# One inference step of a two-layer hybrid decoder: the dt projection made from raw rows, among the first tiles' products

## The chip, the cores and the metric

The kernel runs on one core of a Trainium2 chip. Its time is the device time of one execution in microseconds (us); the time shown is the median of three runs, 936.38 us, with a lowest of 936.22 and a highest of 937.31.

The engines are named as in the profile: PE is the matrix engine and PEld its weight loads, DVE the vector engine, ACT the scalar (activation) engine, POOL the third elementwise engine, SP the queue that issues most transfers. Each engine works through its own instructions in the order in which they stand in its queue, and waits there for semaphores of the others.

## The reference, cut to what matters

The model has one state-space layer (Mamba-2 SSD, mixer A) and one dilated-attention layer (mixer B). 512 prompt rows and 8 x 4 sample rows, 544 in all, of width 1024 go through both. The change lies at the start of mixer A:

```python
u = rmsnorm(h, g_norm) @ w_in
z      = u[..., :SSM_INNER]                        # 2048 columns
xbc    = u[..., SSM_INNER:SSM_INNER + CONV_DIM]    # 3072 columns: x, B, C
dt_raw = u[..., SSM_INNER + CONV_DIM:]             # 32 columns, one per head
...                                                # causal conv over xbc, silu
dt = softplus(dt_raw + dt_bias)
a  = -exp(a_log)
y, s_final = ssd_scan(xs * dt[..., None], dt * a, bm, cm, ssm_init)
```

`rmsnorm(x, g)` is `x * rsqrt(mean(x*x) + eps) * g`. Its first factor is one number per row, so a product with a weight may be made from `x * g` (raw rows) and multiplied by that number afterwards. The scan needs `dt` of all heads before its first chunk of 128 rows: every decay in it comes from sums of `dt * a`.

## The kernel before, in words

Activations lie transposed: 128 of the 1024 features on the partitions, eight such pieces (k = 0 to 7), and the 544 rows along the free axis. The rows are handled in two halves, columns 0 to 255 and 256 to 543 (256 prompt rows and the 32 sample rows). A weight tile is 1024 x 128. Each product is made in three passes of a rounded format to keep the precision of full floats: the weight is split into `whi` (ACT, L205 or L440) and `wlo` = raw - `whi` (DVE, L206 or L444), the rows into a high and a low part, and PE sums `whi` x high, `whi` x low and `wlo` x high. One tile is so 24 products for each half.

**The first five tiles** (16, 20 and 0 of the x|B|C columns, then z 0 and z 1) are made from raw rows, since the norm isn't known yet: `raw(i, ks)` splits `x * g` into `xh` and `xl` (ACT L389, DVE L393), `passes` makes the products, and `scaled_in`, `scaled_in2` and `z_raw` multiply the results by the norm `rs_x`. Squares for the norm are made on ACT (`x_square`), added on DVE (`x_add`), summed over partitions on PE (`x_sums`, the tile `ms`), and the root is spread over the partitions by one more product (`rp`), copied to `rs_x` by ACT. Meanwhile DVE and ACT make the normed rows: `norm(i, ks)` is for each k an `x_mul` (DVE L385, in place: `x` is overwritten by the normed row), an `x_high` (ACT L398, `nh`) and an `x_low` (DVE L402, `nl`). **All later tiles** are made from `nh` and `nl`. Order is fixed by hand in this stretch: PE's products are pinned, and instructions under `hold` keep their places; the rest is placed by a scheduler with priorities (weight splits have high priority).

**The dt projection** (`dt_proj`, L558 to L566) comes after the fifth tile: for each k, four products of the 1024 x 32 weight `wd` with 128 prompt rows each, and four with 8 sample rows each, in full float format. Group j of rows (j = 0 to 3) goes to partitions 32j to 32j+31 of one PSUM tile `dp`, that is to its own quarter of PE's columns. It reads the normed rows `x` in place, so it needs `x_mul` of both halves. `dt_chain` (L568 to L602) then makes softplus, decays and their exponentials out of `dp` in some 20 small steps of 136 columns on DVE and ACT, writes them to memory (`aed`) and prepares `dgs`, from which PE spreads decays (`spread_decays`, `dx`) and transposes (`tp`, `tq`) inside the stream of tiles.

After that a loop runs over the units of the scan (`ssm_chunk`, `ssm_quad`) while a generator, `filler_a`, feeds the remaining tiles to PE between them: tiles 6, 7 and 8 (x 1, x 2, x 3), then `tok_transposes`, tile 9, and after the first six products of half 0 of tile 10 the first chunk, whose transposes `xp` read the convolved and activated x tiles 0 to 3 (`xs`, DVE L644 and L645 behind ACT's tanh L643). Below, "tile 6" is the first tile from normed rows. PSUM has two rotating pools: `pj` (three banks, for the tiles' sums) and `pss` (five banks, for all else). Weight splits have two buffers each, so `whi` of a tile can be made when PE is through with the tile two before it.

Of the kernel before, what the change touches and what calls it, by code (L numbers as in the profile page):

```python
# [12 lines left out]
F32 = mybir.dt.float32  # L13
F32R = mybir.dt.float32r
AF = mybir.ActivationFunctionType
ALU = mybir.AluOpType
# [3 lines left out]
SEQ = 512  # L20
# [6 lines left out]
KD = D // 128  # L27
# [100 lines left out]
def tile_yoco_step(  # L128
# [6 lines left out]
    nc = tc.nc  # L135
    dma = nc.sync.dma_start
# [6 lines left out]
    hold = tc.keep_in_program_order  # L143

    def mm(*a, **k):
        pin(nc.tensor.matmul(*a, **k))  # L146
# [13 lines left out]
    def pj(name, cols=512):  # L160
        return psum.tile([128, cols], F32, name=name, tag="pj", bufs=3)

    def pss(name, shape=(128, 512)):
        return psum.tile(list(shape), F32, name=name, tag="ss", bufs=5)
# [29 lines left out]
    def fetch_w(src):  # L194
        raw = wpool.tile([128, 8, 128], F32, name="wraw", bufs=3)
        dma(raw, src)
        return raw
# [108 lines left out]
    w_raw = [fetch_w(w_in[0])]  # L306
    load_x(1, 0, HA)
    w_raw.append(fetch_w(w_in[1]))
    for i in range(2):
        load_x(i, HA, T)  # L310
    w_raw.append(fetch_w(w_in[2]))

    x_h = [half("xh0", F32R), half("xh1", F32R)]
    x_l = [half("xl0", F32R), half("xl1", F32R)]
    wd = wk.tile([128, 8, 32], F32, name="wd", bufs=1)
    dma(wd, w_dt)
    dcs = ac.tile([128, 2], F32, name="dcs")
    dma(dcs, dconst)
    tm = half("tm").rearrange("p a b -> p (a b)")
# [38 lines left out]
    xdg = tm[:, 1600:1600 + T]  # L358
    halves = ((0, HA), (HA, T))

    def x_square(i):
        c0, c1 = halves[i]
        for h_ in range(2):
            hold(nc.scalar.activation(sqx[h_][:, :, c0:c1], x_t[h_][:, :, c0:c1], AF.Square))

    def x_add(i):
        s0_, s1_ = (sqx[j][:, :, halves[i][0]:halves[i][1]] for j in range(2))
        hold(nc.vector.tensor_tensor(s0_, s0_, s1_, op=ALU.add))
        hold(nc.vector.tensor_tensor(s0_[:, 0:2], s0_[:, 0:2], s0_[:, 2:4], op=ALU.add))
# [12 lines left out]
    def x_mul(k, i):  # L382
        c0, c1 = halves[i]
        xk = part(x_t, k, c0, c1)
        hold(nc.vector.scalar_tensor_tensor(xk, xk, g_a[:, k:k + 1], rs_x[:, c0:c1], op0=ALU.mult, op1=ALU.mult))  # L385
# [10 lines left out]
    def x_high(k, i):  # L396
        c0, c1 = halves[i]
        hold(nc.scalar.activation(part(n_h, k, c0, c1), part(x_t, k, c0, c1), AF.Copy))  # L398

    def x_low(k, i):  # L400
        c0, c1 = halves[i]
        hold(nc.vector.tensor_tensor(part(n_l, k, c0, c1), part(x_t, k, c0, c1), f32(part(n_h, k, c0, c1)), op=ALU.subtract))  # L402

    def passes(p, w, i, high=True, low=True, between=None):
        c0, c1 = halves[i]
        hi, lo = w
        o = p[:, 0:c1 - c0]
        for k in range(KD if high else 0):
            mm(o, hi[:, k, :], part(x_h, k, c0, c1), start=k == 0, stop=False)
            mm(o, hi[:, k, :], part(x_l, k, c0, c1), start=False, stop=False)  # L410
            if between:
                between(k)
        for k in range(KD if low else 0):
            mm(o, lo[:, k, :], part(x_h, k, c0, c1), start=False, stop=k == KD - 1)
# [21 lines left out]
    def w_high(i):  # L436
        hi = wpool.tile([128, 8, 128], F32R, name="whi", bufs=2)
        lo = wpool.tile([128, 8, 128], F32R, name="wlo", bufs=2)
        w_first[i] = hi, lo
        hold(nc.scalar.activation(hi, w_raw[i], AF.Copy))  # L440

    def w_low(i):
        hi, lo = w_first[i]
        hold(nc.vector.tensor_tensor(lo, w_raw[i], f32(hi), op=ALU.subtract))  # L444

    def raw(i, ks):
        for k in ks:
            x_raw_h(k, i)
            x_raw_l(k, i)

    def norm(i, ks):
        for k in ks:
            x_mul(k, i)
            x_high(k, i)
            if k:
                x_low(k - 1, i)

    def next_raw(i):
        w_raw.append(fetch_w(w_in[i]))
        w_high(i)  # L460

    raw(0, range(4))
    w_high(0)
    raw(0, range(4, KD))
    w_high(1)
    w_low(0)
    w_low(1)
    x_square(0)
    pa, pb = [pj("pa"), pj("pb")], [pj("pa")]
    passes(pa[0], w_first[0], 0, low=False)  # L470
    passes(pa[1], w_first[1], 0, low=False)
    passes(pa[0], w_first[0], 0, high=False)
    passes(pa[1], w_first[1], 0, high=False)
    x_add(0)
# [5 lines left out]
    def spread_a(k):  # L480
        if k == 4:
            hold(nc.scalar.copy(rs_x[:, 0:HA], spread()[:, 0:HA]))

    passes(pb[0], w_first[0], 1, between=spread_a)
    x_square(1)
    cbs = [scaled_in(first[0], pa[0]), scaled_in(first[1], pa[1])]
    x_add(1)
    n_h = [half("nh0", F32R), half("nh1", F32R)]
    n_l = [half("nl0", F32R), half("nl1", F32R)]
    pb.append(pj("pb"))  # L490
    w_high(2)
    norm(0, range(2))
    passes(pb[1], w_first[1], 1)
    sums = x_sums(1)
    spread = rstd_fin(*sums, later=True, keep=hold)
# [50 lines left out]
                x_low(KD - 1, 1)  # L546
    x_h, x_l = n_h, n_l


    t0, t1, t2, t3, t4 = (tm[:, 136 * i:136 * i + 136] for i in range(1, 6))  # L550
    pads = tm[:, 816:1200].rearrange("p (a b) -> p a b", b=128)
    dgs = tm[:, 1200:1584].rearrange("p (a b) -> p a b", b=128)
    tok = ac.tile([128, 6, 3, NH], F32, name="tok")
    dec = ac.tile([128, 12, NH], F32, name="dec")
    nega = ac.tile([128, 1], F32, name="nega")
    dp = [None]

    def dt_proj():  # L558
        dp[0] = pss("dp")
        for k in range(KD):  # L560
            for j in range(4):
                xk = x_t[k // 4][:, k % 4, :]
                o = dp[0][32 * j:32 * j + 32]
                mm(o[:, 0:128], wd[:, k, :], xk[:, 128 * j:128 * j + 128], start=k == 0, stop=False, skip_group_check=True)
                mm(o[:, 128:136], wd[:, k, :], xk[:, SEQ + 8 * j:SEQ + 8 * j + 8], start=False, stop=k == KD - 1,
                   skip_group_check=True)  # L566

    def dt_chain():  # L568
        nc.vector.tensor_scalar(t0, dp[0][:, 0:136], dcs[:, 0:1], None, op0=ALU.add)
        nc.vector.scalar_tensor_tensor(t1, t0, -1.0, t0, op0=ALU.mult, op1=ALU.min)  # L570
        nc.scalar.activation(t2, t1, AF.Exp)
        tc.keep_in_program_order(nc.scalar.activation(nega, dcs[:, 1:2], AF.Exp))
        nc.vector.tensor_scalar(t3, t2, 1.0, None, op0=ALU.add)
        nc.scalar.activation(t1, t3, AF.Ln)
        nc.vector.tensor_scalar(t3, t3, -1.0, 1e-30, op0=ALU.add, op1=ALU.max)
        nc.vector.reciprocal(t3, t3)
        nc.vector.tensor_tensor(t1, t1, t2, op=ALU.mult)
        nc.vector.tensor_tensor(t1, t1, t3, op=ALU.mult)
# [12 lines left out]
        nc.vector.tensor_tensor(t4, t4, t0, op=ALU.mult)  # L591
        t23 = tm[:, 136 * 3:136 * 5].rearrange("p (i c) -> p i c", i=2)
        dma(aed[:].rearrange("i r c -> r i c"), t23[:, :, 0:128])
        dma(sed0[:], t23[:, :, 128:136])
        for i in range(2):
            dma(dap(sed, i * NH * 32, [[32, NH], [8, 4], [1, 8]]), dap(sed0, 8 * i, [[16, NH], [16 * NH, 4], [1, 8]]))
        for i, c in enumerate((127, 131, 135)):
            nc.vector.tensor_scalar(dgs[:, i, :], ident, t3[:, c:c + 1], None, op0=ALU.mult)
        nc.gpsimd.memset(pads, 0.0)
        for i, s in enumerate((t2, t0, t4)):  # L600
            for r in range(2):
                thrice(pads[:, i, 64 * r:64 * r + 64].rearrange("p (b c) -> p b c", c=32), s[:, 128:136])  # L602
# [63 lines left out]
        return xs_t[ti // 4][:, ti % 4, :]  # L666

    def conv_tile(ti, w):
        pa, pb = pj("pa"), pj("pb")
        yield from proj_steps(pa, [w], x_h, x_l, 0, HA)  # L670
        yield from proj_steps(pb, [w], x_h, x_l, HA, T)
        conv(ti, pa[:, 0:HA], pb[:, 0:HB], conv_dst(ti))
# [226 lines left out]
    units = [(f, (g, i)) for g in range(4) for f, i in  # L899
             ((ssm_chunk, 0), (ssm_chunk, 1), (ssm_quad, 0), (ssm_chunk, 2), (ssm_chunk, 3), (ssm_quad, 1))]  # L900
    conv_out(first[0], cbs[0], conv_dst(first[0]))
    dt_proj()
    dt_chain()
    conv_out(first[1], cbs[1], conv_dst(first[1]))
    conv_out(first[2], cbs[2], conv_dst(first[2]))
# [737 lines left out]
    for u in range(len(units) + LA + 2):  # L1643
        i = u - LA
# [111 lines left out]
```

## Time and profile before

| | us |
|---|---|
| median of three runs | 936.38 |
| the profiled execution, its own time | 932.79 |
| its span on the core | 931.0 |
| PE busy (98% of the span) | 912.7 |
| DVE busy (74%) | 684.8 |
| ACT busy (53%) | 490.0 |
| POOL busy (17%) | 161.1 |

The span counts from the first instruction of the program to the last; what the execution's time has beyond it, 1.8 us, lies around it. The profiled execution is some 3.6 us shorter than the median. In the rows of the profile a group of instructions stands with the line of the kernel that issued it; since all products go through one helper, PE's rows have the helper's line (L146, transposes L149) and are told apart by the names of what they write and read. A timeline row gives start, duration, engine, line, operation, operands and how many instructions it merges; in brackets the engine's idle time before it and what ended that.

### The profile page before, as it was taken

Reading aid. Unit: us, or ns where it says so; the run is one execution under the profiler, and the core shown is the slowest. Engines: PE = TensorE matmul, PEld = TensorE weight load, DVE = VectorE, ACT = ScalarE, POOL = GpSimd, SP = SyncE. Lnnn points to the kernel's source line nnn. Section 1 sums busy time; section 2 is a strip of 40 time slices with the busy share of each in tenths; the row PEclk is TensorE's granted clock in tenths of the full one; section 3 lists DMA queues with packets and bytes.
Section 4 is the critical chain, followed back from the end, with each engine's and each line's share of the span. In section 5 each row is a group of like instructions: output and inputs, shape, how many; then the busy total and the mean of one; then the engine's idle time right before and its main releaser. Section 6 shows DMA issues by size and latency. Waiting matters only on the chain.

```text
span 931.0 us, 21867 instructions
## 1 busy us (share of the span) xinstructions
PE 912.7 (98%) x8667; PEld 843.5 (91%) x8667; DVE 684.8 (74%) x1434; ACT 490.0 (53%) x1140; POOL 161.1 (17%) x206
## 2 busy tenths in 40 slices
PE   8999999999999999999999999999999999999996
PEld 8999889888788889999999999988988888888996
DVE  6998799989799899554588436866777766777732
ACT  6668656755665655322255213555555555567642
POOL 2020344533533633111001000000000000000021
PEclk9999999999999999999999999999999999999999
DMA  8224265355356433636286556767868767785411
GB/s 295 92 74 141 102 213 184 129 177 176 115 192 211 157 112 106 170 114 226 78 286 211 185 167 192 259 206 250 277 198 252 268 227 255 249 269 176 150 49 49
DMA packets 80557, 168.48 MB, mean 181 GB/s; under 512 B 19974, under 2 KB 37720, under 8 KB 79944
## 3 DMA queue, kind: packets, MB, share of 16 engines
q1 hardware_dynamic: 73768, 154.60, 50.9%
q10 hardware_dynamic: 5616, 9.75, 2.8%
q0 software_dynamic: 1072, 2.74, 1.1%
q8 instruction: 68, 1.11, 0.5%
q14 instruction: 33, 0.27, 0.1%
HBM read 141.14 MB, written 25.93 MB: 179 GB/s over the span
## 4 chain that ended last, share of the span: by engine, by line
PE 84%; DVE 9%; DMA 3%; ACT 2%; issue 1%; SPq 0%; DVEq 0%; ACTq 0%
PE pa L146 34%; PE pb L146 28%; PE sp L146 3%; PE so L146 3%; PE pv L146 2%; PE s L146 2%; DVE co L641 1%; DVE wlo L206 1%; PE yd L146 1%; DMA m<-aed 1%; PE csp L146 1%; PE w L149 1%; PE ptp L149 1%; PE xp L149 1%; DMA vc<-cv 1%; DVE v L699 1%
## 5 line engine op out<-in xcount | busy, mean ns | idle before, releaser
L206 DVE TENSOR_TENSOR wlo<-wraw,whi 128x1024 fp32r<-128x1024 f32 x69 | 89.3, 1294 | 49.5 <-ACT whi L205 48.8
L205 ACT ACTIVATE whi<-wraw 128x1024 fp32r<-128x1024 f32 x69 | 72.9, 1057 | 100.0 <-PE pb L146 59.4
L146 PE MATMUL pa<-bq,whi 128*128 128x272 f32 x512 | 103.2, 296 | 0.0
L146 PE MATMUL pb<-nl,whi 128*128 128x288 f32 x280 | 83.7, 299 | 0.0
L146 PE MATMUL pb<-nh,wlo 128*128 128x288 f32 x280 | 83.2, 297 | 0.0
L146 PE MATMUL pb<-nh,whi 128*128 128x288 f32 x280 | 83.1, 297 | 0.0
L146 PEld LDWEIGHTS pa<-bq,whi 128*128 128x128 f32 x512 | 81.3, 189 | 0.8
L146 PE MATMUL pa<-nh,whi 128*128 128x256 f32 x280 | 80.9, 289 | 0.0
L146 PE MATMUL pa<-nl,whi 128*128 128x256 f32 x280 | 80.6, 288 | 0.0
L146 PE MATMUL pa<-nh,wlo 128*128 128x256 f32 x280 | 79.9, 285 | 0.0
L146 PE MATMUL pb<-bq,whi 128*128 128x272 f32 x384 | 77.2, 296 | 0.6 <-DVE kv L1221 0.5
L146 PE MATMUL pa<-bq,wlo 128*128 128x272 f32 x256 | 74.3, 290 | 0.0
L641 DVE SCALAR_TENSOR_TENSOR co<-cb,cvp,co 128x568 f32<-128x568 f32 x72 | 65.4, 911 | 1.3 <-ACT co L639 0.7
L146 PEld LDWEIGHTS pb<-bq,whi 128*128 128x128 f32 x384 | 60.8, 189 | 1.9 <-DVE kv L1221 0.8
L1280 ACT ACTIVATE whi<-wraw 128x512 fp32r<-128x512 f32 x64 | 40.1, 627 | 36.4 <-PE pb L146 16.6
L146 PEld LDWEIGHTS pb<-nl,whi 128*128 128x128 f32 x280 | 52.6, 188 | 4.4 <-issue 4.4
L146 PE MATMUL pb<-bq,wlo 128*128 128x272 f32 x192 | 55.5, 289 | 0.0
L146 PEld LDWEIGHTS pa<-nh,whi 128*128 128x128 f32 x280 | 53.6, 191 | 1.9 <-issue 1.9
L146 PEld LDWEIGHTS pa<-nl,whi 128*128 128x128 f32 x280 | 53.6, 191 | 1.4 <-issue 1.4
L146 PEld LDWEIGHTS pb<-nh,wlo 128*128 128x128 f32 x280 | 52.8, 188 | 2.2 <-issue 2.2
L146 PEld LDWEIGHTS pa<-nh,wlo 128*128 128x128 f32 x280 | 53.5, 191 | 0.9 <-issue 0.9
L146 PEld LDWEIGHTS pb<-nh,whi 128*128 128x128 f32 x280 | 52.7, 188 | 0.8 <-issue 0.8
(401 smaller groups left out, 2778.7 us busy)
## 6 DMA issues: line engine op xcount, KB each, us to landing
wraw<-w_in SPq DMA_DIRECT2D x40, 512.0 KB
kc<-ck SPq DMA_DIRECT2D x32, 640.0 KB
vc<-cv SPq DMA_DIRECT2D x32, 640.0 KB
wraw<-wb SPq DMA_DIRECT2D x32, 512.0 KB
s<-s SPq DMA_DIRECT2D x32, 256.0 KB
m<-aed SPq DMA_DIRECT2D x16, 512.0 KB
ssmS<-s ACTq DMA_DIRECT2D x32, 256.0 KB
wraw<-w_out SPq DMA_DIRECT2D x16, 512.0 KB
```

The source lines that it names most:

```text
L146: pin(nc.tensor.matmul(*a, **k))
L149: pin(nc.tensor.transpose(*a))
L205: a = nc.scalar.activation(hi, raw, AF.Copy)
L206: b = lo_eng.tensor_tensor(lo, raw, f32(hi), op=ALU.subtract)
L641: nc.vector.scalar_tensor_tensor(o, cb[:, k:k + n], cvp[:, ti, k:k + 1], o, op0=ALU.mult, op1=ALU.add)
L699: nc.vector.scalar_tensor_tensor(vi, xs_t[g][:, i, :], dsk[:, 4 * g + i:4 * g + i + 1], vi, op0=ALU.mult, op1=ALU.add)
L1280: nc.scalar.activation(hi, src[p][j], AF.Copy)
```

## The change

- `wd` is fetched earlier: behind the weights of the second tile, ahead of the second halves of `x`. DVE multiplies it by the norm's weight `g_a`.
- `dt_proj` is gone. Its products are made from raw `x` (not yet overwritten) in two parts. `dt_rows(0, k)`: two products of 128 rows (j = 0, 1) behind each pair of `whi` products of the second tile's half 0. `dt_rows(1, k)` and `dt_samples(k)`: two of 128 rows (j = 2, 3) and four of 8 rows behind each pair of the first tile's half 1. So 32 products of 128 rows and 32 of 8 rows are made as before, in 16 visits.
- `dp` is taken from `pss` at the start and kept until `dt_chain` reads it. There `rs_x` is first gathered into the layout of `dp` by eight ACT copies (`rsd`), and DVE multiplies.
- The squares of half 1 are split about the copy of `rs_x`, and two `x_mul` are put ahead of `x_add(1)`.
- The sums of tile 6 (`ti == 1`) go to `pss` banks instead of `pj`.

```diff
     w_raw.append(fetch_w(w_in[1]))
+    wd = wk.tile([128, 8, 32], F32, name="wd", bufs=1)
+    dma(wd, w_dt)
     for i in range(2):
         load_x(i, HA, T)
...
+    dp = pss("dp")
+
+    def dt_rows(i, k):
+        xk = x_t[k // 4][:, k % 4, :]
+        for j in range(2 * i, 2 * i + 2):
+            mm(dp[32 * j:32 * j + 32, 0:128], wd[:, k, :], xk[:, 128 * j:128 * j + 128], start=k == 0, stop=k == KD - 1,
+               skip_group_check=True)
+
+    def dt_samples(k):
+        xk = x_t[k // 4][:, k % 4, :]
+        for j in range(4):
+            mm(dp[32 * j:32 * j + 32, 128:136], wd[:, k, :], xk[:, SEQ + 8 * j:SEQ + 8 * j + 8], start=False,
+               stop=k == KD - 1, skip_group_check=True)
+
     raw(0, range(4))
     w_high(0)
     raw(0, range(4, KD))
     w_high(1)
+    hold(nc.vector.tensor_tensor(wd, wd, g_a[:, :, None].to_broadcast([128, 8, 32]), op=ALU.mult))
     w_low(0)
...
-    passes(pa[1], w_first[1], 0, low=False)
+    passes(pa[1], w_first[1], 0, low=False, between=lambda k: dt_rows(0, k))
...
     def spread_a(k):
         if k == 4:
             hold(nc.scalar.copy(rs_x[:, 0:HA], spread()[:, 0:HA]))
-
+        dt_rows(1, k)
+        dt_samples(k)
+
+    x_square(1, (0,))
     passes(pb[0], w_first[0], 1, between=spread_a)
-    x_square(1)
+    x_square(1, (1,))
     cbs = [scaled_in(first[0], pa[0]), scaled_in(first[1], pa[1])]
+    x_mul(0, 0)
+    x_mul(1, 0)
     x_add(1)
...
-    norm(0, range(2))
+    for k in range(2):
+        x_high(k, 0)
+    x_low(0, 0)
     passes(pb[1], w_first[1], 1)
...
     def dt_chain():
-        nc.vector.tensor_scalar(t0, dp[0][:, 0:136], dcs[:, 0:1], None, op0=ALU.add)
+        rsd = t4
+        for j in range(4):
+            rows = slice(32 * j, 32 * j + 32)
+            nc.scalar.copy(rsd[rows, 0:128], rs_x[rows, 128 * j:128 * j + 128])
+            nc.scalar.copy(rsd[rows, 128:136], rs_x[rows, SEQ + 8 * j:SEQ + 8 * j + 8])
+        nc.vector.tensor_tensor(t0, dp[:, 0:136], rsd, op=ALU.mult)
+        nc.vector.tensor_scalar(t0, t0, dcs[:, 0:1], None, op0=ALU.add)
...
     def conv_tile(ti, w):
-        pa, pb = pj("pa"), pj("pb")
+        bank = pss if ti == 1 else pj
+        pa, pb = bank("pa"), bank("pb")
...
     conv_out(first[0], cbs[0], conv_dst(first[0]))
-    dt_proj()
     dt_chain()
```

How this moves instructions, at three places. First PE, in the second tile's half 0 as the change has it (`xh`, `xl` are raw rows, `pb` the tile's sums); before, the rows of `pb` followed each other without the rows of `dp`:

```order
L146 MATMUL pb<-xh_115,whi 128x256
L146 MATMUL pb<-xl_117,whi 128x256
L146 MATMUL dp<-x_69,wd 32x128 x2
L146 MATMUL pb<-xh_115,whi 128x256
L146 MATMUL pb<-xl_117,whi 128x256
L146 MATMUL dp<-x_69,wd 32x128 x2
```

Eight such visits stand there, and eight, with four 32x8 products more each, in the first tile's half 1. Second PE at the end of tile 5 as it was before, where `dt_proj` began; it ran through 64 such rows, up to the first `nh` row of tile 6:

```order
L146 MATMUL pa<-xh_113,wlo 128x288 x4
L146 MATMUL pa<-xh_114,wlo 128x288 x4
L146 MATMUL dp<-x_69,wd 32x128
L146 MATMUL dp<-x_69,wd 32x8
L146 MATMUL dp<-x_69,wd 32x128
```

Now the last `wlo` row of tile 5 has tile 6 right behind it:

```order
L146 MATMUL pa<-xh_115,wlo 128x288 x4
L146 MATMUL pa<-xh_116,wlo 128x288 x4
L146 MATMUL pa<-nh_362,whi 128x256
L146 MATMUL pa<-nl_364,whi 128x256
L146 MATMUL pa<-nh_362,wlo 128x256
```

Third DVE, ahead of the first chunk, before (`co` are steps of the convolution, `xs` activated x tiles, the last pair x 3; `xdt` the first step of the chunk):

```order
L641 SCALAR_TENSOR_TENSOR co<-cb,cvp,co 128x568 x3
L644 SCALAR_TENSOR_TENSOR xs<-cb,co 128x512
L645 SCALAR_TENSOR_TENSOR xs<-cb,co 128x32
L206 TENSOR_TENSOR wlo<-wraw,whi 128x1024
L739 TENSOR_TENSOR xdt<-xp,tok 128x512
```

and as the change has it:

```order
L658 SCALAR_TENSOR_TENSOR co<-cb,cvp,co 128x568 x3
L206 TENSOR_TENSOR wlo<-wraw,whi 128x1024
L661 SCALAR_TENSOR_TENSOR xs<-cb,co 128x512
L662 SCALAR_TENSOR_TENSOR xs<-cb,co 128x32
L849 TENSOR_TENSOR ms<-as,tok 128x128 x2
```

The split of tile 11's weights (`wlo`) stands ahead of `xs` of x 3 now, and behind it before.

More of the change, by code (lines that the diff above doesn't have):

```diff
@@ L314, in tile_yoco_step @@
     x_l = [half("xl0", F32R), half("xl1", F32R)]
-    wd = wk.tile([128, 8, 32], F32, name="wd", bufs=1)
-    dma(wd, w_dt)
     dcs = ac.tile([128, 2], F32, name="dcs")
@@ L359, in tile_yoco_step, with x_square @@
     halves = ((0, HA), (HA, T))
-    def x_square(i):
+    def x_square(i, hs=(0, 1)):
         c0, c1 = halves[i]
-        for h_ in range(2):
+        for h_ in hs:
             hold(nc.scalar.activation(sqx[h_][:, :, c0:c1], x_t[h_][:, :, c0:c1], AF.Square))
@@ L555, in tile_yoco_step @@
     nega = ac.tile([128, 1], F32, name="nega")
[L556 to L566, printed above, removed]
-    def dt_chain():
-        nc.vector.tensor_scalar(t0, dp[0][:, 0:136], dcs[:, 0:1], None, op0=ALU.add)
+    def dt_chain():
+        rsd = t4
[5 more added lines that the diff above has]
+        nc.vector.tensor_scalar(t0, t0, dcs[:, 0:1], None, op0=ALU.add)
         nc.vector.scalar_tensor_tensor(t1, t0, -1.0, t0, op0=ALU.mult, op1=ALU.min)
```

## The prediction

> **What bounds the kernel now.** I read the page's busy shares and its chain first, then PE's waits, then timelines of the first 80 us on PE, DVE and ACT.
>
> ```profile
> PE 912.7 (98%) x8667; PEld 843.5 (91%) x8667; DVE 684.8 (74%) x1434; ACT 490.0 (53%) x1140; POOL 161.1 (17%) x206
> PE 84%; DVE 9%; DMA 3%; ACT 2%; issue 1%; SPq 0%; DVEq 0%; ACTq 0%
> ...
> PE dp L146 <- DVE x L385: 2.4, 4, 1.5
> PE up L146 <- DVE xdd L741: 1.7, 1, 1.7
> PE xp L149 <- DVE xs L644: 1.7, 2, 1.2
> PE yd L146 <- DVE cbs L818: 0.6, 1, 0.6
> ```
>
> PE is the bound, so what it computes and where it waits decide. The longest waits are those of `dp`, on `x_mul`. The timeline of PE there:
>
> ```profile
> 44.14 1.53 PE L146 MATMUL dp<-x,wd 128*32 128x128 f32 x66
> 47.14 0.48 PE L146 MATMUL dp<-x,wd 128*32 128x8 f32 x16 [1.46 <-DVE x L385]
> 49.94 0.48 PE L146 MATMUL pa<-nh,whi 128*128 128x256 f32 x1
> 57.60 0.28 PE L146 MATMUL pa<-nh,whi 128*128 128x256 f32 x1
> ```
>
> `dp` holds PE for 5.8 us (44.14 to 49.94), and tile 6 ends at 57.60. Who works meanwhile is in the stretches (columns: PE, PEld, DVE, ACT, POOL busy, the granted clock, DMA share, GB/s):
>
> ```profile
> 27.00:51.00 24.00, 21.41 (x266) 20.52 (x265) 23.73 (x53) 14.03 (x29) 0.00 (x0) 0.98 0.35 111
> 50.10:53.40 3.30, 3.30 (x16) 3.30 (x17) 2.86 (x8) 2.35 (x5) 0.26 (x1) 0.50 0.00 0
> 51.00:77.00 26.00, 26.00 (x198) 25.68 (x197) 22.97 (x46) 20.80 (x53) 5.43 (x11) 0.95 0.34 102
> ```
>
> From 27 to 51 us DVE is full (23.73 of 24), up to 77 nearly so (22.97 of 26): behind PE stands DVE. And after the idling in `dp` PE's clock was 0.50 for a while: 16 products in 3.3 us, 0.21 each, where later ones take 0.12, so 1.5 us were lost.
>
> **What it removes.** Without `dp` at that place PE goes from tile 5 to tile 6 at 44.14. Half 0 takes 24 x 0.12 = 2.8 us; half 1 needs `nl` of each k, which DVE makes one after the other:
>
> ```profile
> 27.04 0.42 DVE L427 TENSOR_TENSOR cb<-pa,rstd 128x256 f32<-128x256 f32 x1 [0.55 <-ACT rstd L501]
> 50.35 0.46 DVE L402 TENSOR_TENSOR nl<-x,nh 128x288 fp32r<-128x288 f32 x1
> ```
>
> The last lands at 50.81, and three products, 0.4 us, are left: tile 6 would end at 51.25 in place of 57.60, a gain of 6.35 us. It waits about 1 us in short pieces there, so I keep the clock whole. DVE's own chain from L427 to that `nl` has the same instructions in the same order in the change.
>
> **What it adds on PE.** 16 visits to `dp` inside products that follow each other without a pause. Their price is nowhere in the trace; the nearest rows are other changes between full-width products (128\*128) and column pieces (128\*32 and 128\*64):
>
> ```profile
> 589.14 0.41 PE L146 MATMUL pb<-bq,whi 128*128 128x272 f32 x2
> 589.39 0.29 PE L146 MATMUL pb<-bq,wlo 128*128 128x272 f32 x1
> 589.61 0.75 PE L146 MATMUL sp<-kv,qp 128*32 128x32 f32 x18
> ...
> 102.94 1.09 PE L146 MATMUL yd<-m,xdt 128*64 128x128 f32 x16
> 103.96 0.39 PE L146 MATMUL pa<-nl,whi 128*128 128x256 f32 x1
> 104.19 0.29 PE L146 MATMUL pa<-nh,wlo 128*128 128x256 f32 x1
> 104.31 0.28 PE L146 MATMUL pa<-nh,whi 128*128 128x256 f32 x1
> ```
>
> `yd` is the same form as `dt_rows`: pairs of products in separate columns, 128 wide, each in two passes. 16 instructions took 1.02 us, 0.128 for each pass of a pair, so 0.26 for the two passes of one visit. Entering costs: `sp` starts 0.22 behind the product before it, where 0.12 is usual, so 0.1. Leaving costs: the first product behind `yd` takes 0.23 in place of 0.12, so 0.1. A start and an end that `yd` spreads over eight passes fall on each visit here, 0.04 as I take it. So 0.50 for a visit of half 0. The four narrow products: `dp` took at most 1.53 / 4 = 0.38 for each k with all eight products, 0.12 over a bare pair; I take 0.07, so 0.57 in half 1. The sum is 8 x 0.50 + 8 x 0.57 = 8.6 us. The bounds: streams alone, 8 x 0.26 + 8 x 0.31 = 4.6; start and end at 0.1 and the narrow ones at 0.1, 8 x 0.56 + 8 x 0.66 = 9.8. I stay near the upper one because the rows show an edge at entry and at exit.
>
> The Trainium skill bears on this: TensorEngine Tiling, Key Properties, says that changing the tiling mode, not just the tile, drains the engine. The rows of `sp` and `yd` agree, with 0.1 us on either side. By that rule the 32 changes of mode are all paid, which is the 8.6; without it the sum would be the 4.6.
>
> Is it hidden? In the second tile's half 0 and the first tile's half 1 PE's rows were:
>
> ```profile
> 13.61 1.11 PE L146 MATMUL pb<-xh,wlo 128*128 128x256 f32 x8
> 14.56 1.05 PE L146 MATMUL ms<-inv,sqx 128*128 128x1 f32 x8
> ...
> 16.61 0.29 PE L146 MATMUL pa<-xh,whi 128*128 128x288 f32 x1
> 17.39 0.40 PE L146 MATMUL pa<-xl,whi 128*128 128x288 f32 x1 [0.50 <-DVE xl L393]
> ...
> 25.82 0.75 PE L146 MATMUL rp<-tm,ones 128*128 128x288 f32 x2 [0.18 <-DVE tm L276]
> ```
>
> No pause up to `ms`, one of 0.78 - 0.13 = 0.65 at 17.39, which the visits cover, and from there none up to the sums of half 1 and `rp`. DVE's L427 hangs on that `rp`. So L427, and with it the whole full DVE queue, comes later by S = 8.6 - 0.65 = 7.9 us (3.9 to 9.1).
>
> **The other edits** I cost at nothing.
>
> ```profile
> GB/s 295 92 74 141 102 213 184 129 177 176 115 192 211 157 112 106 170 114 226 78 286 211 185 167 192 259 206 250 277 198 252 268 227 255 249 269 176 150 49 49
> ...
> 12.43 1.81 ACT L389 ACTIVATE xh<-x,gn 128x288 fp32r<-128x288 f32 x4
> ```
>
> The product `wd` x `g_a` is 128x256 on DVE, about 0.4 us (L427's row has that width), ahead of `wlo` that PE needs only behind the first visits, now later. `wd`'s 128 KB ahead of `x`'s second halves: in the trace ACT starts on these (12.43) without a wait; if they came late, it would be 0.44 us at the page's 295 GB/s. The eight copies of `rsd` stand on ACT behind `rs_x` and ahead of the next `nh`; ACT was busy 14 of 24 us there; uncovered, 1 us. The two `x_mul` put forward fill DVE idle time before L427 and don't shorten what follows it. Other banks for tile 6: PE waited for none here, so neither gain nor loss.
>
> **Where the stall goes.** PE's own account is +7.9 - 6.35 = +1.6 us at the end of tile 6; but DVE is 7.9 late, and PE needs it at the first chunk:
>
> ```profile
> 76.39 0.69 DVE L644 SCALAR_TENSOR_TENSOR xs<-cb,co 128x512 f32<-128x512 f32 x1 [1.07 <-ACT cb L643]
> 77.00 0.19 DVE L645 SCALAR_TENSOR_TENSOR xs<-cb,co 128x32 f32<-128x32 f32 x1
> 78.80 1.23 DVE L206 TENSOR_TENSOR wlo<-wraw,whi 128x1024 fp32r<-128x1024 f32 x1 [1.61 <-ACT whi L205]
> 79.95 0.68 DVE L739 TENSOR_TENSOR xdt<-xp,tok 128x512 f32<-128x512 f32 x1
> ...
> 77.73 1.04 ACT L205 ACTIVATE whi<-wraw 128x1024 fp32r<-128x1024 f32 x1
> ...
> 78.04 0.60 PE L149 MATMUL xp<-ident,xs 128*128 128x128 f32 x4
> ```
>
> `xs` was done at 77.1, 0.9 before `xp`. From the last `nl` to there were 26.2 us, with 22.97 of DVE work. The change puts into this piece the product with `rsd` (0.3) and, by its order, the `wlo` of tile 11 ahead of `xs` (1.15, as 78.80 to 79.95): at least 24.4, at most the old 26.2. I take 25.4, since the new order also lets DVE wait for a `whi` that ACT can only make when PE has left tile 9. `xs` is so done at 50.81 + 7.9 + 25.4 = 84.1, and `xp` is 6.1 us later than before (5.1 to 6.9 for this S); PE, 1.6 late itself, waits the other 4.5 us, part of them at `dx`, whose input DVE also makes late in this piece (before, PE came to `dx` 1.7 us behind it):
> ```profile
> 67.27 0.67 DVE L598 TENSOR_SCALAR tm<-ident,tm 128x128 f32<-128x128 f32 x3
> ...
> 69.65 0.81 PE L146 MATMUL dx<-tm,ones 128*128 128x384 f32 x2
> ```
>
> Whatever S is, that order makes PE wait: `whi` 1.05, `wlo` 1.15 and `xs` 0.7 now follow the end of tile 9, and `xp` comes 1.0 behind it, so at least 1.9.
>
> **What is given back.** Further on PE itself waited for DVE (`up`, `xp`, `yd` of the first fence: 1.7, 1.7, 0.6, all at 212 to 287 us). DVE, which has one `wlo` more behind it, is less late than PE then. I give back the first of these waits, 1.2 us (bounds 0 and 3.9). The sum: +6.1 - 1.2 = +4.9 us. The profiled execution would go from 932.79 to 937.7; it lies 3.6 under the median, and the same step on the median gives 936.4 + 4.9 = **941.3 us**.
>
> **The rivals.**
> - Bare streams: a visit costs what its passes take, since pieces of PE's columns start on their own. S is then 3.9 and the first chunk late by 3.9 + 25.4 + 50.81 - 78.04 = 2.1 (1.1 to 2.9); less 1.2, the time is **937.3**. For it speaks that `dp`'s own groups ran at 0.38 us for each k; against it the edges at 589 and 104 us.
> - The visits are hidden, and it is faster: PE's products of the first stage are not what the rest waits for, and S is 0.5 or less. `xs` is then done early enough for `xp` to come 1.3 us sooner than before, the rest of the 6.35 is waited away there, and 1.2 is given back later: 2.5 faster, **933.9**. The point is S under 1.1, below which the two together pass 0.2%. Against it: the sums `ms` follow the products without a pause.
> - The clock: a wait of 3 to 4 us at `xp` brings the clock to 0.50 as that of `dp` did, and 1.5 us more go, **942.8**. The Trainium skill has such a rule (TensorE: Matmul & The Clock Gate, Part 1): half clock after an idle window of about 3.4 us. In the trace pauses of 1.2 and 1.7 us left the clock whole, and `dp` didn't, so the trace agrees as far as it goes.
> - All is given back: the later waits take up 3.9 us, +2.2, **938.6**. For it: they are all waits on DVE. Against it: DVE was full there, too:
>
> ```profile
> 212.00:290.00 78.00, 74.95 (x613) 66.85 (x613) 71.00 (x106) 47.99 (x121) 29.73 (x32) 1.00 0.48 158
> ```
>
> **How the numbers follow.** Chances: the forecast 0.46, the clock 0.15, all given back 0.13, bare streams 0.13, hidden 0.13. A difference under 0.2% (1.9 us) can't be told from none here. Slower by more: 0.46 + 0.15 + most of 0.13 = 0.70; faster 0.13; the same 0.17. The range goes from 935.0, which takes in bare streams, to 945.5, with S at 9.1, the late end of the piece on DVE, the slow clock and nothing but 1.2 given back; the hidden case and the tails, under 2 in 10, are outside. The forecast's own range is 939 to 944.
>
> **What would show it.** Right: visits with starts 0.45 or more from the product before to the one behind beyond the usual step; `ms` of half 0 at about 18.5 us in place of 14.56; L427 at about 35 us; no `dp` between tiles 5 and 6; a wait of PE at `xp` for `xs` of 2 to 5 us at about 80 to 84 us, with `wlo` ahead of `xs` on DVE. Wrong: L427 before 31 us (visits cheap), `xp` without a wait (DVE was not behind), or PE's later waits gone altogether.

## The result, and the profile after

| | before | after |
|---|---|---|
| median, us | 936.38 (934.25 to 937.31, five runs) | 946.73 (942.85 to 949.84, five runs) |
| the profiled execution | 932.79, span 931.0 | 949.09, span 947.3 |
| starts of L427 / of the last transpose of the first `xp` | 27.04 / 78.37 | 34.99 / 87.47 |

The change makes the kernel slower by 10.4 us: 1.0113 times the time before, 95% interval 1.0091 to 1.0136. The forecast was 941.3 (935.0 to 945.5): the sign was right, the size less than half of what came.

The page of the changed kernel, PE's busy time and the granted clock in 40 slices:

```profile
PE 922.5 (97%) x8667; PEld 848.5 (90%) x8667; DVE 684.4 (72%) x1436; ACT 492.5 (52%) x1148; POOL 161.5 (17%) x206
PEclk9999999998999999999999999999999999999999
PE 82%; DVE 9%; DMA 4%; ACT 3%; issue 1%; SPq 0%; DVEq 0%; ACTq 0%
```

PE has the same 8667 products, yet 9.8 us more busy time; the clock of the tenth slice is 0.8. PE's waits now:

```profile
PE xp L149 <- DVE xs L661: 4.9, 2, 2.9
PE pb L146 <- ACT cb L343: 3.5, 1, 3.5
PE s L146 <- DMA kc<-ck: 1.8, 3, 0.8
PE up L146 <- DVE xdd L759: 1.6, 1, 1.6
```

The 2.4 us of `dp` are gone; 3.5 us on a PSUM bank (L343 is ACT's copy of a tile's sums) and 3.2 us more at `xp` have come. The timelines of PE and DVE through the first stage show the predicted part:

```profile
10.58 0.38 PE L146 MATMUL pb<-xh,whi 128*128 128x256 f32 x1
10.80 0.28 PE L146 MATMUL pb<-xl,whi 128*128 128x256 f32 x1
11.01 0.41 PE L146 MATMUL dp<-x,wd 128*32 128x128 f32 x4
11.35 0.39 PE L146 MATMUL pb<-xh,whi 128*128 128x256 f32 x1
...
18.78 0.95 PE L146 MATMUL ms<-inv,sqx 128*128 128x1 f32 x8
20.41 0.40 PE L146 MATMUL pa<-xh,whi 128*128 128x288 f32 x1
20.87 0.45 PE L146 MATMUL dp<-x,wd 128*32 128x128 f32 x12
21.25 0.40 PE L146 MATMUL pa<-xh,whi 128*128 128x288 f32 x1
...
34.99 0.42 DVE L427 TENSOR_TENSOR cb<-pa,rstd 128x256 f32<-128x256 f32 x1 [0.61 <-ACT rstd L525]
...
52.01 0.28 PE L146 MATMUL pa<-nh,whi 128*128 128x256 f32 x1
58.83 0.40 PE L146 MATMUL pb<-nl,whi 128*128 128x288 f32 x1 [0.31 <-DVE nl L402]
```

From one `xh` product to the next are 0.77 us in half 0 (11.35 - 10.58) and 0.84 in half 1, where two bare products take 0.235 and 0.262: a visit costs 0.54 and 0.58. Entry takes 0.21 us (10.80 to 11.01), and the first product behind is followed at 0.22 to 0.24. L427 starts 7.95 us later; S, the lateness of DVE's queue, was put at 7.9. PE stands 1.5 us later at the end of tile 6 (58.83 against 57.33 for the same product), as forecast. Then come the rows that the prediction doesn't have:

```profile
67.09 0.68 ACT L660 ACTIVATE cb<-co 128x568 f32<-128x568 f32 x1 [0.66 <-DVE co L658]
69.28 0.19 ACT L341 COPY cb<-zero 128x3 f32<-128x3 f32 x1 [1.51 <-DVE CT L662]
71.33 0.36 ACT L343 COPY cb<-pa 128x256 f32<-128x256 f32 x1
...
67.73 1.22 DVE L206 TENSOR_TENSOR wlo<-wraw,whi 128x1024 fp32r<-128x1024 f32 x1
69.01 0.18 DVE L662 SCALAR_TENSOR_TENSOR CT<-cb,co 128x32 f32<-128x32 f32 x1
...
71.75 0.40 PE L146 MATMUL pb<-nh,whi 128*128 128x288 f32 x1 [3.52 <-ACT cb L343]
84.97 0.49 PE L149 MATMUL xp<-ident,xs 128*128 128x128 f32 x3
87.47 0.33 PE L149 MATMUL xp<-ident,xs 128*128 128x128 f32 x1 [2.01 <-DVE xs L661]
```

Tile 8's half 1 is ready to start at 68.2 and stands until 71.75, since its bank still holds tile 7's half 0. ACT copies that at 71.33, because its queue stood before: for L658 (a tap of the convolution), then for L662, the end of the C tile, without which there is no free `cb` buffer for tile 6. And L662 stands on DVE behind a `wlo`. So this too is a wait for DVE's queue, passed on by ACT. Behind the stop the clock drops, and again further on:

```profile
72.30:75.60 3.30, 3.30 (x16) 3.30 (x15) 3.30 (x10) 1.28 (x3) 1.63 (x3) 0.50 0.38 106
222.50:229.20 6.70, 6.02 (x28) 6.03 (x29) 5.35 (x10) 5.03 (x13) 0.22 (x1) 0.50 0.37 114
270.30:273.60 3.30, 3.30 (x16) 3.30 (x15) 3.29 (x7) 1.87 (x3) 0.00 (x0) 0.50 0.28 112
```

(From:to, length, busy time of PE, PEld, DVE, ACT, POOL, then the granted clock.) Before, there was one such stretch ahead of the last microseconds, that behind `dp`.

The same products set side by side in the two traces give the account of the profiled executions, +16.3 us: 1.5 late at the end of tile 6; 5.3 behind the stop for the bank; 6.9 behind the slow clock; 9.1 at the first `xp`; 10.8 behind the next long wait at `xp` (2.88 us at 223.18, in place of 1.23 at 212.39); 13.5 and 14.9 behind the slow stretches at 222 and 270; 14.3 at 301; 16.3 behind waits for `kc` transfers from 675 on. The medians differ by less, 10.4: of the five runs each lists its mean granted clock, from 0.994 (942.85 us) to 0.989 (949.84). With (1 - clock) x span, the time lost to a slow clock, taken off, they are 937.2 to 939.6; the medians of the kernel before, in the runs beside the experiments, come to 930 to 931 that way, with some 4 to 6 us lost. So about 8 us of the 10.4 are not the clock, and 2 to 3 are.

### The profile page after: what moved, and what is told of

Read it like the earlier page. It is cut to its first block, busy times and chain, and to the rows that moved or that the text cites. A ratio compares the mean times of both kernels' runs of the same rounds, so it can differ in the third digit from the quotient of the medians.

```text
span 947.3 us, 21875 instructions
## 1 busy us (share of the span) xinstructions
PE 922.5 (97%) x8667; PEld 848.5 (90%) x8667; DVE 684.4 (72%) x1436; ACT 492.5 (52%) x1148; POOL 161.5 (17%) x206
## 4 chain that ended last, share of the span: by engine, by line
PE 82%; DVE 9%; DMA 4%; ACT 3%; issue 1%; SPq 0%; DVEq 0%; ACTq 0%
PE pa L146 33%; PE pb L146 28%; PE sp L146 3%; PE pv L146 2%; PE so L146 2%; PE s L146 2%; DVE wlo L206 2%; DVE co L658 2%; DMA kc<-ck 1%; DMA m<-aed 1%; PE yd L146 1%; DVE vl L888 1%; PE csp L146 1%; PE w L149 1%; PE ptp L149 1%
## 5 line engine op out<-in xcount | busy, mean ns | idle before, releaser
L658 DVE SCALAR_TENSOR_TENSOR co<-cb,cvp,co 128x568 f32<-128x568 f32 x72 | 64.2, 896 | 1.5 <-ACT co L656 0.9
```

The source lines that it names most:

```text
L658: nc.vector.scalar_tensor_tensor(o, cb[:, k:k + n], cvp[:, ti, k:k + 1], o, op0=ALU.mult, op1=ALU.add)
```

## The experiments

The expectations call DVE VectorE, ACT ScalarE and POOL GpSimd. All times are medians, and every ratio is to the kernel before, run beside it on the same chip; a difference in us is the ratio less 1 times 936.

**Fewer visits, fewer changes.** Three kernels make S small without touching the rest. One keeps the first visit of each half only:

```diff
-        for j in range(2 * i, 2 * i + 2):
+        for j in range(2 * i, 2 * i + 2) if k == 0 else ():
```

> The changed kernel with only the first of the eight visits in each half; the other 7/8 of the dt products are left out. Visits as the cause: L427 at about 27.5 us (S about 0.5), no stop for a bank at tile 8, little or no wait at the first xp, and 932 to 936 us. The new order of VectorE's queue and the banks as the cause, whatever the visits: the stop for the bank and the wait at xp stay at 2 us or more each, and the time stays above 940.

One makes each half's products in a block:

```diff
-    passes(pa[1], w_first[1], 0, low=False, between=lambda k: dt_rows(0, k))
+    passes(pa[1], w_first[1], 0, low=False)
+    for k in range(KD):
+        dt_rows(0, k)
```

> The changed kernel with the same dt products, each half's in one block behind the products among which the eight visits stood. If a visit costs its entry and exit, the blocks cost 8 x 0.26 + 0.2 = 2.3 and 8 x 0.31 + 0.2 = 2.7 us, S is about 4.3 in place of 7.9, and the time 938 to 942. If a visit costs its streams alone, S stays near 8 and the time at 946.

And one, run last as a test of what the others had shown, makes all of them in one block, four groups of PE's columns at a time:

> The changed kernel with all dt products of the raw rows in one block behind the first tile's half 1, and nothing else altered (no GpSimd work). L427 then starts about 2.8 us later than in the kernel before, as in the run named e11_one_block_pool. If the time follows that delay alone, as a line through the runs with one visit (0.4 us late, +2.2) and with all sixteen (7.95 us late, +10.6) has it, the time is 2.2 + 2.4 x 1.12 = 4.9 us over the kernel before: 940 to 942. If the number of PE's changes between the two kinds of product matters beyond this delay, it is at or below the kernel before.

The blocks in the timelines of PE (two blocks, then one):

```profile
12.99 1.94 PE L146 MATMUL dp<-x,wd 128*32 128x128 f32 x32
14.86 0.62 PE L146 MATMUL pa<-xh,wlo 128*128 128x256 f32 x3
...
22.03 2.42 PE L146 MATMUL dp<-x,wd 128*32 128x128 f32 x96
24.38 0.40 PE L146 MATMUL pb<-xh,whi 128*128 128x288 f32 x1
```

```profile
20.27 2.44 PE L146 MATMUL dp<-x,wd 128*32 128x128 f32 x128
```

The eight visits of half 0 cost 4.3 us, the same products in one block 2.2 (the pairs of passes take 0.22 each, plus one entry and exit). Seven changes to and fro are thus worth 2.1 us, 0.30 each: the prediction's 0.24 a visit for entry, exit and start was a little low, and the streams a little high. The Trainium skill has the rule that the prediction weighed (TensorEngine Tiling (Array Packing), Key Properties: a change of mode drains the engine). These runs agree that the change costs, 0.3 us for in and out. How the delay passes on:

| products | S: start of L427 less 27.04 | last transpose of `xp` less 78.37 | median, us | ratio, interval | in us |
|---|---|---|---|---|---|
| first visits only | 0.42 | 1.55 | 937.68 | 1.0023 (1.0007 to 1.0039) | +2.2 |
| one block | 2.78 | 4.97 | 940.07 | 1.0038 (1.0025 to 1.0051) | +3.6 |
| two blocks | 4.58 | 6.76 | 942.58 | 1.0065 (1.0043 to 1.0087) | +6.1 |
| 16 visits (the change) | 7.95 | 9.10 | 946.73 | 1.0113 (1.0091 to 1.0136) | +10.6 |

`xp` is late by S and 1.1 to 2.2 us more, and the whole time follows S at about 1.1 us for each: S is neither hidden nor given back. (The 2.2 are those of the middle rows, whose profiled executions had 6.8 us of half clock ahead of `xp`; the other two had 3.4.) The one block had been put at 940 to 942 by the line through the others and came at 940.07; its +3.6 (2.3 to 4.8) lies 1.3 under the line. The two blocks had been put at 938 to 942 and came a little above. Even with S at 0.4 and 7/8 of the products missing the kernel isn't faster than before. With the time lost to a slow clock taken off as above, the rows lie, in the table's order, 0.6 below the kernel before and 3.1, 3.7 and about 8 us above it: what the first row loses is the clock. PE's waits in that one:

```profile
PE pb L146 <- ACT cb L343: 3.5, 1, 3.5
PE xp L149 <- DVE xs L661: 2.9, 2, 2.0
```

The stops are all there, though DVE is hardly late. So neither expectation came as a whole: the stops stayed, and the time fell to 937.7 all the same. The stops are not made by the visits: they are what has become of the 6.35 us that PE gained. What the visits add is that PE and DVE are both later by S when it stops. This kernel also holds all the other edits of the change (the gathered norm, the moved instructions, DVE's order), so that they and the removal together are worth no more than the 2.2.

**What the removal is worth.** In the kernel before, `dp` is cut to the first of its eight k (`for k in range(1)`), first alone, then with tiles 6 and 7 in the `pss` banks, so that no tile waits for a bank:

> The kernel before with only the first eight of dp's 64 products, at the same place (7/8 of the dt products are left out). That is what the removal is worth alone. If PE's account sets the end: dp takes 0.4 us, no wait, whole clock, so 936.4 - 5.6 = about 931. By the prediction's hidden case (VectorE stands behind PE, xs not before 77 us) only 1.3 us come through at the first xp and up to 1.2 are waited away later: 934 to 936.

> The kernel before with the first eight of dp's 64 products (7/8 of the dt products are left out) and tiles 6 and 7 in the other banks. The stop of 6.55 us at tile 7 goes. VectorE as the bound: xs still done at 76 to 78 us, PE waits 4 to 6 us at the first xp, and the time is 934 to 937. PE as the bound: no long wait in its place, and 930 to 932.

938.15 us, ratio 1.0026 (1.0006 to 1.0045), above both ranges that I had given, and 934.25, ratio 0.9986 (0.9967 to 1.0005). PE's waits of the two, and the first `xp` of the second:

```profile
PE pb L146 <- ACT cb L343: 6.6, 1, 6.6
```

```profile
PE dx L146 <- DVE tm L598: 3.9, 1, 3.9
...
78.47 0.33 PE L149 MATMUL xp<-ident,xs 128*128 128x128 f32 x1 [0.47 <-DVE xs L644]
```

PE is 6.4 and 6.2 us early at the end of tile 6. In the first it stops 6.55 us for tile 6's bank at 60.74, and the clock drops for 6.8 us behind it; in the second it stops at `dx`, the clock drops for 3.4, and `xp` comes 0.1 us later than before. The time that `dp` cost on PE was time in which PE would have waited. A variant that needs nothing left out moves `dp`, made of normed rows as before, behind tile 6, with tiles 6 and 7 in the `pss` banks and the first chunk 24 products later; these lines are the move:

```diff
-    dt_proj()
-    dt_chain()
...
+    run(48)
+    dt_proj()
+    dt_chain()
```

> The kernel before with dp's products, of the normed rows as before, one tile later (behind tile 6), tiles 6 and 7 in the other banks, and the first chunk half a tile (24 products) later. dp waits for nothing there, so PE gains its 2.4 us of waits and 1.5 us of slow clock; if the 24 products keep PE busy until xs is done (about 78 us), the time is 931 to 934; if VectorE has fallen behind by dt's later chain, PE waits at xp and the time is 936 or more.

936.23 us, ratio 1.0007 (0.9990 to 1.0023): no difference. It stops 2.7 us at `tq`, for POOL's copies that follow dt's chain on DVE.

**The banks.** The change with tile 6 back in `pj`, and the change with tiles 6 and 7 in `pss`:

```diff
-        bank = pss if ti == 1 else pj
+        bank = pj                              # the first
+        bank = pss if ti in (1, 2) else pj     # the second
```

> The changed kernel with tile 6's sums back in the three banks that all other tiles use. By the prediction's step (neither gain nor loss) the time stays where the changed kernel is, 946.7 within 1 us. By the bank theory (a tile finds no free bank because ScalarE's copies stand behind the late VectorE) the stop only moves: tile 7's half 1 at about 62 us needs the bank of tile 6's half 0, which ScalarE copied at 69.5, so PE stops 5 to 8 us there, in place of 3.5 us at 71.8, the clock drops there, and the time is 948 to 951.

> The changed kernel with the sums of tiles 6 and 7 in the other banks, so that tile 8's half 1 finds a free one. If the stop for a bank (3.5 us and about 1.5 of slow clock at 71.8 us) is a cost of its own, it goes, and the time is about 5 us less, 941 to 943. If VectorE's lateness is what stands behind it, PE comes to the first xp about 5 us sooner and waits there for xs, which is at most 1.5 us sooner (VectorE's own idle time behind the stop): a wait of 5 to 7 us at xp, and 944.5 to 947.

946.29 us, ratio 1.0119 (1.0091 to 1.0148), and 944.31, ratio 1.0092 (1.0070 to 1.0113). In the first PE stops 6.55 us at tile 7 instead of 3.52 at tile 8, as the bank theory had it, but the time stays, as the prediction's step had it; in the second it stops at `dx` instead:

```profile
PE dx L146 <- DVE tm L615: 3.8, 1, 3.8
```

The bank decides where PE stops, and hardly for how long. The second lies between the two ranges that I had given; it may gain 2 us, within the intervals of each other. DVE's order differs in it, too: the `wlo` of tile 11 stands behind `xs` again, at 85.59, and the last transpose of the first `xp` is 7.3 us late in place of 9.1.

**More work for PE meanwhile.** The second of these, with the first chunk 48 products later (`OFF` from 8 to 56):

> The changed kernel with the banks of two tiles as in the run named e5_banks_two_tiles, and one whole tile more of projection products (48) ahead of the first chunk, so that PE has work while VectorE is late. If the change costs what PE waits for the late VectorE: no stop ahead of xp and a wait below 1 us there, and 937 to 940, of which the visits' own 1.5 us on PE stay. If something else costs the time: 944 or more.

959.65 us, ratio 1.0250 (1.0225 to 1.0274): far worse than the 937 to 940 that would have followed from PE's wait for the late DVE. The wait at the first `xp` is gone, and those of the later units have grown:

```profile
PE up L146 <- DVE xdd L759: 4.2, 2, 2.2
PE pa L146 <- DVE vl L888: 4.1, 3, 2.0
PE dx L146 <- DVE tm L615: 3.8, 1, 3.8
PE pb L146 <- DVE uz L695: 3.1, 1, 3.1
```

By the runs' mean clocks about 7 of the 15 us that it takes more than that second kernel are slow clock. A chunk brings work for DVE as well as for PE. My reading is that later chunks crowd DVE's work into what is left, so that DVE is short of time in the whole stage; no run tests it.

**Less work for DVE.** First the `wlo` of tiles 6 to 9 were given to GpSimd, the profile's POOL (`lo_eng=nc.gpsimd`): in the change, in the kernel before, with `dp` behind tile 6 (the first chunk at its old place), and with the one block (tiles 6 and 7 in the `pss` banks).

> The changed kernel with the wlo of tiles 6 to 9 made on GpSimd, which takes 4 x 1.2 us out of VectorE's queue ahead of the first xs. If VectorE's queue is the chain that carries the visits' delay into xp, xs is 3 to 4.5 us sooner, the stop at tile 8 is below 1 us, and the time 942 to 943.5. If PE's products or the banks are the chain, the stops stay and the time is 946 to 947.5.

> The kernel before with the same four wlo on GpSimd. In it PE reaches the first xp 0.9 us behind xs, so VectorE's earlier end has nothing to give there: 935 to 937. A gain of 2 us or more would say that VectorE's queue bounds the kernel before beyond the first chunk, too.

> The kernel before with dp's products behind tile 6, tiles 6 and 7 in the other banks, the first chunk at its old place, and the wlo of tiles 6 to 9 on GpSimd. PE is 3.9 us sooner by the waits and the slow clock that go, and VectorE up to 4.8 us by the wlo that go: if these two are what binds, the time is 931 to 934; if the stop at dx or tq stays (2.7 to 3.9 us in the runs without GpSimd's help), 935.5 to 937.

> The changed kernel with all dt products of the raw rows in one block behind the first tile's half 1 (all four column groups together, about 0.35 us for each k, so S about 2.5 in place of 7.9), tiles 6 and 7 in the other banks and the wlo of tiles 6 to 9 on GpSimd. S passes on in full and VectorE gains up to 4.8 us: 932 to 936. If the clock and the stops behind xp set the time whatever S is: 940 or more.

950.62 us, ratio 1.0166 (1.0136 to 1.0196); 939.19, 1.0038 (1.0018 to 1.0058); 947.95, 1.0132 (1.0103 to 1.0161); 945.12, 1.0109 (1.0078 to 1.0140). All are slower than their nearest like without it, by 5.0, 3.6, 12 and 6.6 us (the last two differ from it in the chunk's place or the banks as well), and the timelines of POOL and DVE of the first say why:

```profile
46.64 2.38 POOL L206 TENSOR_TENSOR wlo<-wraw,whi 128x1024 fp32r<-128x1024 f32 x1 [29.76 <-ACT whi L205]
65.14 2.79 POOL L206 TENSOR_TENSOR wlo<-wraw,whi 128x1024 fp32r<-128x1024 f32 x1 [2.37 <-ACT whi L205]
...
46.89 3.22 DVE L444 TENSOR_TENSOR wlo<-wraw,whi 128x1024 fp32r<-128x1024 f32 x1
65.59 2.42 DVE L590 TENSOR_SCALAR tm<-tm 128x136 f32<-128x136 f32 x1
```

While GpSimd works, the DVE instruction that meets it stands: L444 takes 3.22 us where it takes 1.22 alone, L590 2.42 in place of 0.22. The same happened at each of the four in this run: some 2.0 to 2.2 us longer. So these runs took nothing from DVE; they held it up for some 2 us where a `wlo` costs it 1.2. They say nothing for the kernel with a relieved DVE, but they add delay to its queue by another way, and again it comes out at the end: +5.0 us on the change, +3.6 on the kernel before.

So the four `wlo` were left out instead, and `whi` used in their place:

```diff
         a = nc.scalar.activation(hi, raw, AF.Copy)
+        if no_lo:
+            return hi, hi
```

> The changed kernel with the wlo of tiles 6 to 9 left out (their products take whi a second time, so that PE's work is the same and their low part is missing). It takes 4 x 1.2 us out of VectorE's queue without giving them to GpSimd, which in the runs with wlo on GpSimd held VectorE up. If VectorE's queue carries the visits' delay into the first xp, xp is 6 us late or less in place of 9.1, and the time 941 to 943.5. If PE's own products, the banks or the clock carry it, the time stays at 945 to 947.

> The kernel before with the same four wlo left out. In it PE reaches the first xp 0.9 us behind xs, so the first chunk comes no sooner: 935 to 937. If VectorE's lead is kept to the later waits (1.2 us at 212, 1.7 at 256): down to 933.

> The kernel before with the first eight of dp's 64 products, tiles 6 and 7 in the other banks, and the wlo of tiles 6 to 9 left out: both PE's work and VectorE's are less. If the two together are what binds up to the first chunk, xp is 3 to 5 us sooner than before and the time 930 to 933; if the later waits take it all back, 934 to 936 as without the second step.

| four `wlo` less on DVE | median, us | ratio, interval | without that step |
|---|---|---|---|
| the change | 938.06 | 1.0030 (1.0012 to 1.0048) | 1.0113 |
| the kernel before | 932.31 | 0.9964 (0.9944 to 0.9985) | 1 |
| the kernel before, `dp` cut, other banks | 931.69 | 0.9956 (0.9939 to 0.9972) | 0.9986 |

In the change 4.9 us less on DVE are worth 7.8 us. PE's waits and the first `xp` of that kernel (L345 is there what L343 is elsewhere):

```profile
PE pb L146 <- ACT cb L345: 1.3, 1, 1.3
PE xp L149 <- DVE xs L663: 1.2, 2, 0.8
...
80.39 0.60 PE L149 MATMUL xp<-ident,xs 128*128 128x128 f32 x4
```

The stop for the bank falls from 3.5 to 1.3, the wait at the first `xp` goes, the clock stays whole up to 257 us, and `xp` is 2.35 us late (80.39 against 78.04) though S is still 8.3. The time is below the 941 to 943.5 that I had expected. Part of this the kernel before gains as well. With the same relief it is 3.4 us faster, and its first `xp` comes 3.3 us sooner, where I had expected it no sooner:

```profile
74.78 0.60 PE L149 MATMUL xp<-ident,xs 128*128 128x128 f32 x4
```

Like against like, the change makes `xp` 5.6 us late with the relief and 9.1 without, and costs 6.2 us in place of 10.6. The 4.4 us between them, with some 3.4 either way, are what the relief of DVE takes from the change alone: DVE's queue carries at least that part of the visits' delay. The 6.2 that are left, with DVE still 8.3 us late at L427, were not taken apart. In the kernel before DVE is behind, too, and part of `dp`'s wait there was its lateness (0.8 us are left of the 2.4). With DVE relieved, cutting `dp` adds only 0.7 us, within the intervals.

No version that computes everything was faster than the kernel before.

## Why the prediction was wrong

**Right.** The price of a visit (0.50 and 0.57; 0.54 and 0.58 measured), `ms` at 18.78 (18.5), S (7.9; 7.95), PE at the end of tile 6 (+1.6; +1.5), DVE's piece from L427 to the last `nl` with the same length in both kernels (23.8 us), a wait at `xp` with `wlo` ahead of `xs`. That S came out to 0.05 us is in part luck: the 16 visits cost 9.0 us in place of 8.6, and 1.0 of that rather than 0.65 did not reach L427. Bare streams and hidden visits, the two rivals on the cheap side, fall with these.

**Wrong: "I take 25.4"**, the length of DVE's piece from the last `nl` to `xs`, with "at most the old 26.2". The stretches (after, before, then the kernel with the first visits only; the third number behind the length is DVE's busy time):

```profile
58.77:87.52 28.75, 23.16 (x167) 22.41 (x168) 24.84 (x52) 23.16 (x60) 4.93 (x11) 0.94 0.38 113
```

```profile
50.81:77.19 26.38, 26.38 (x200) 26.06 (x199) 23.35 (x49) 20.99 (x54) 5.43 (x11) 0.95 0.34 103
```

```profile
51.23:79.97 28.74, 23.16 (x167) 22.41 (x168) 24.84 (x51) 23.16 (x60) 4.94 (x11) 0.94 0.39 113
```

DVE's work grew by 1.5 us, a `wlo` and the product with `rsd`, as the sum had it. But I took DVE's idle time for slack that a late queue uses up, and it grew, from 3.0 to 3.9 us. Lateness is not what made it grow: with S at 0.42 the piece has the same 28.74 us, the same work and the same idle time as with S at 7.95. So S moved the piece as a whole, and a late DVE won nothing back in it. The length comes from what those two kernels share. Cutting `dp` out of the kernel before, without the new order, already makes the piece 28.30 us, with PE's stop for a bank in it; in the change with tiles 6 and 7 in `pss` and `wlo` behind `xs` it is 26.56. How much is the stop and how much the order no run tells apart. In the prediction's terms, DVE was to win back 1.8 of its 7.9 us by `xp`, and lost 1.15 more: `xp` was 9.1 us late, not 6.1. That is 3.0 of the missing 5.5 us.

**Wrong: "I give back the first of these waits, 1.2 us".** It was not given back there. The waits behind the first chunk are for DVE, and DVE stayed as late as PE: in the profiled execution the wait of 1.23 us became 2.88. Only 0.6 came back later, at 301. Over the four kernels of the first table, S came out in full. That is the other 1.2, and the rival "all is given back" fell with it.

**Wrong: the clock.** I kept it whole at tile 6, which was right, and gave the slow clock 0.15 with one stretch at `xp`. It came behind the stop for the bank and behind the waits at 222 and 270. By the runs' mean clocks it took 2 to 3 us more than before: a mechanism that I had as a rival, in other places. The rival's condition, a wait of 3 to 4 us, was too strict as well: the window ahead of the slow stretch at 50 us before held 1.4 us of idling. These three terms are more than the missing 5.5 us together, since the 9.1 at `xp` may hold up to 1.6 us of slow clock, and the median execution has fewer slow stretches than the profiled one. (The top of the range, 945.5, is 0.7 above what its own terms add up to, 936.4 + 9.1 + 26.2 + 50.81 - 78.04 + 1.5 - 1.2 = 944.8; the median lies above both.)

**Right for a wrong reason: "Other banks for tile 6: neither gain nor loss".** In the sum the banks are indeed worth nothing that the runs could measure. The reason, that PE waited for none before, was empty: in the kernel before `dp` held PE up just long enough for ACT to free them. Removing it turned its wait into that for a bank.

**Half right: the gain of 6.35 us.** PE got it at tile 6 and lost it by the first chunk: with `dp` cut and the visits' cost absent `xp` was 0.1 us later than before with the other banks, and 2.4 with the old ones. I had called DVE full in that stretch, in the first part of the prediction, and yet booked `dp`'s removal and the delay of L427 as two terms of one sum on PE. What the runs say is that the first term is zero, as far as they can measure, and the second counts in full.

## What to carry to other kernels

Ask first which engine's queue is late in the stretch, and price a change by what it does to the start of that queue: here 1 us more at L427 was 1 us more at the end, while 6 us less on the busiest engine were worth nothing. Idle time inside a nearly full queue was no slack: a late start moved the whole stretch and left its length as it was. To tell the two apart, set the same stretch of a kernel with a small delay beside it. A wait that was removed turned up at the next shared resource (a bank, a buffer, a transpose's input). Small products in another part of the matrix engine's columns belong in one block: between full-width products each visit cost 0.3 us beyond its streams.

## What the runs showed of the hardware

**The clock falls without a whole idle window.** The changes of the granted clock in a trace lie multiples of 3.413 us apart (in the changed kernel 72.25, 222.43, 270.22). In the 18 traces of this study, between 10 and 900 us, a window of that grid at whole clock was always followed by half clock if PE idled for 1.66 us or more in it (28 cases), never if it idled for 0.35 to 1.0 us (130 cases); in between it was so in 13 of 38. So a wait of 1.6 us can cost 1.7 us more, by where it falls on the grid. Here is `up` in the changed kernel and in the kernel before, with what followed there:

```profile
269.12 0.61 PE L146 MATMUL up<-xr,btr 32*128 32x512 f32 x2 [1.59 <-DVE xdd L759]
```

```profile
255.71 0.61 PE L146 MATMUL up<-xr,btr 32*128 32x512 f32 x2 [1.66 <-DVE xdd L741]
...
256.00:259.00 3.00, 3.00 (x23) 2.75 (x22) 3.00 (x5) 2.09 (x5) 0.00 (x0) 1.00 0.52 169
```

The first lay in one window, and 270.30 to 273.60 ran at 0.50. The second was cut in two, 0.83 us on each side, and the clock stayed whole. It is part of the spread between executions of one kernel: over 109 runs of the kernel before, taking off the time lost to the clock brings the standard deviation from 2.1 to 1.3 us. The Trainium skill has the free-running window of 3413 ns (TensorE: Matmul & The Clock Gate, Part 1), and the grid agrees; half clock "after ≥1 idle window", as it says there, doesn't: here about half a window was enough.

**A split on GpSimd stops DVE.** An operation on 128x1024 full floats that met one of GpSimd's took DVE 3.22 us in place of 1.22, and a small one of 136 columns 2.42 in place of 0.22; they ended 1.1 and 0.1 us behind GpSimd's. The Trainium skill has a lock of this kind (SBUF — State Buffer, "SBUF: two separate sides": one shared pair of ports, held for the whole instruction, which a DVE operation with two SBUF inputs needs against a GpSimd one that reads SBUF). The first, with two inputs, agrees; whether the second falls under its other condition, a two-port mode of DVE, no run here shows.
